# A state-space decoder step: VectorE's table, power and scan operands moved from SBUF to PSUM, 12 output tables on VectorE

## The chip, the cores and the metric

One core of one Trainium2 chip runs the whole step as one program. The metric is the device time of that program in microseconds: the median of three runs, with the lowest and the highest beside it. Times inside the program come from one profiled execution.

## What is computed

One inference step of a two-layer decoder on 320 tokens (256 of a prompt, 8 sequences of 8 new tokens). Layer 1 is a state-space layer with complex diagonal states (64 groups of 16 channels, 64 states each) and a squared-ReLU MLP; then one shared key/value projection; layer 2 is block attention and another MLP. The part that the change touches is the state-space layer:

```
dt = exp(log_dt);  A = exp((lam_re + i lam_im) dt)          # per group and state
Bbar = (A - 1) / lam * B                                    # complex, 64 states x 16 channels per group
x[t] = A x[t-1] + Bbar u[t]                                 # scan over time, start state given for the samples
y[t] = Re(C x[t]) + d u[t];   y = gelu(y);   h += glu(y W)
```

After it come only large matrix products (the gated unit, MLP, keys, queries, values, attention, output, MLP).

## The kernel before

**Blocks.** Time is cut into 40 blocks (`NK`) of 8 steps (`L`), 32 of the prompt and 8 of the samples. Three things are built from A, B and C for each of 8 sets `hb` of 4 group pairs: the input table (powers of A times B, `table` with `ADD`, lines 293 to 306, tiles `eb` or `fb`), the kernel inside a block (C times the input table, spread to a Toeplitz matrix), and the output table (powers of A times C, `ftab`, line 311, tiles `fb`). A table is five tensor-by-tensor instructions: three products (lines 299 to 301, one of them into a scratch tile) and a difference and a sum (302, 304 or 305).

**Sets.** The loop over `hb` (line 382) goes in the order 0, 1, 2, 3, 6, 4, 5, 7. For sets 0 to 5 VectorE builds the input table; for 6 and 7 GpSimd does. TensorE transposes the table (line 404), ScalarE copies it out of PSUM (`et`, 405), TensorE multiplies it with the tokens (413) and ScalarE copies the block inputs out (`e`, 416). Three more steps trail behind by one, two and three places (`chunks`): `kernel` (340 to 344), `toeplitz` (353, 354) and `within` (364), whose result either stays in its PSUM bank (`HELD`) or is copied to `ya` (370).

**Powers and scan.** VectorE then completes the powers A^1 to A^8 (`PW`, lines 423 to 426) and, by squaring, A^8, A^16, A^24 and A^32 (`AW`, with a sign-changed copy `AP_`, lines 435 to 440). The scan (lines 449 to 486) runs in two halves of 16 group pairs: `cstep` (455 to 458, four instructions of 128x256) three times, then a serial loop of seven times four instructions of 128x32 (473 to 476, on `z`), then `cstep` three more times; the results go to `st`, the states at the start of each block. GpSimd meanwhile builds the output tables of `FP` (26 of 32 group pairs); VectorE builds those of `FL` (6) after the scan. GpSimd also makes the final states of the samples (`finished`), clears a tile (682) and makes two weight remainders (547).

**The end of the part.** TensorE multiplies `st` with the output tables (line 504), adding to the held banks; for sets not held VectorE adds `ya` (512); ScalarE applies the GELU (513), TensorE transposes (519), ScalarE and VectorE split the result in two (522, 523), and the gated unit's products begin (567 to 569).

**What sets the order.** The program is written in one order and each engine's own queue comes out of a list scheduler that weighs waits; `issue_after` adds a condition. Each engine works its queue strictly in that order. PSUM has eight banks of 128x512, handed out by `Slots`, oldest freed first. One of them (`PF`, line 278) already holds a copy of the first eight powers for the tables of sets 1 to 5; all else that VectorE reads there lies in SBUF.

Of the kernel before, what the change touches and what calls it, by code (L numbers as in the profile page):

```python
# [16 lines left out]
AF = mybir.ActivationFunctionType  # L17
# [14 lines left out]
NEG = -1e30  # L32
FP = (0, 4), (4, 4), (8, 4), (12, 4), (16, 4), (20, 4), (24, 2)
FL = (26, 2), (28, 4)
HELD = (3, 4, 5, 6, 7)
WARM = 18, 25
# [4 lines left out]
MUL, ADD, SUB, MAX, MIN = ALU.mult, ALU.add, ALU.subtract, ALU.max, ALU.min  # L41
# [21 lines left out]
def body(ctx: ExitStack, tc: tile.TileContext, I, O):  # L63
# [22 lines left out]
    tz_, st, ya, yb = (slot(n_, 2624) for n_ in ("tz", "st", "ya", "yb"))  # L86
    Y = [ya[:, i * 512:(i + 1) * 512] for i in range(5)]
    eb = [wpool.tile([128, 1024], F32, name=f"eb{i}", tag="wr") for i in range(4)]
# [153 lines left out]
    def cmulv(out, x, y, ypm, n, w=scr, o2=512):  # L242

        d = [[64, n], [32, 2], [1, 32]]
        t1, t2 = fv(w, 0, d), fv(w, o2, d)
        V.tensor_tensor(t1, fv(x, 0, d), fv(y, 0, [[0, n], [0, 2], [1, 32]]), op=MUL)
        V.tensor_tensor(t2, fv(x, 32, [[64, n], [-32, 2], [1, 32]]), fv(ypm, 0, [[0, n], [32, 2], [1, 32]]), op=MUL)
        return V.tensor_tensor(fv(out, 0, d), t1, t2, op=ADD)


    pm(p1, PW[:, 64:128])
# [25 lines left out]
    cmulv(px[:, 256:512], px[:, 0:256], PW[:, 256:320], p4, 4)  # L277
    PF = B.get()
    e8 = [[64, 8], [1, 32]]
    summed = V.tensor_tensor(fv(px, 512, [[32, 8], [1, 32]]), fv(px, 0, e8), fv(px, 32, e8), op=ADD)  # L280
    A.activation(PF, px[:, 0:512], AF.Copy)


# [23 lines left out]
    xb, xc = (bre, bim, bsum), (cre, cim, csum)  # L307
    prod = yb[:, 0:512]
    held = {}

    def ftab(eng, gp, n, k1):

        return table(eng, fb[gp // 8][:, gp % 8 * 256:(gp % 8 + n) * 256], k1, PW, 64, pws, xc, gp, SUB, n)
# [7 lines left out]

    last = table(V, eb[0], prod, px, 0, px[:, 512:768], xb, 0, ADD)
    P.tensor_tensor(w0, rs0, rs0, op=MUL)
# [57 lines left out]
    for n_, hb in enumerate(order):  # L381
# [6 lines left out]
        if hb < 6:  # L388
            ebt = eb[hb % 4]
            if n_:  # L390
                last = table(V, ebt, prod, PF, 0, px[:, 512:768], xb, g0, ADD)
        else:
            ebt = fb[3][:, (hb - 6) * 1024:(hb - 5) * 1024]
            with tc.issue_after(scaled.ins):
                early = table(P, ebt, scr, px, 0, px[:, 512:768], xb, g0, ADD)
# [24 lines left out]

    B.put(PF)

    with tc.issue_after(last.ins):
        cmulv(PW[:, 192:256], PW[:, 128:192], PW[:, 64:128], p1, 1, fin, 256)
        cmulv(PW[:, 320:576], PW[:, 64:320], PW[:, 256:320], p4, 4, fin, 256)
        powers = V.tensor_tensor(fv(pws, 0, [[32, 8], [1, 32]]), fv(PW, 64, e8), fv(PW, 96, e8), op=ADD)

    for n_ in range(8, 11):
        chunks(n_)
    with tc.issue_after(early.ins):  # L430
        for gp, n in FP:
            tabled = ftab(P, gp, n, scr)
    with tc.issue_after(powers.ins):

        V.tensor_copy(AW[:, 0:64], PW[:, 512:576])
        pm(AP_[:, 0:64], AW[:, 0:64])
        cmulv(AW[:, 64:128], AW[:, 0:64], AW[:, 0:64], AP_[:, 0:64], 1, fin, 256)
        pm(AP_[:, 64:128], AW[:, 64:128])
        cmulv(AW[:, 128:256], AW[:, 0:128], AW[:, 64:128], AP_[:, 64:128], 2, fin, 256)
        pm(AP_[:, 128:256], AW[:, 128:256], 2)  # L440

# [6 lines left out]
    for g0 in (0, 16):  # L448
        def ev(j, sw=False, n=8, step=4):
            return fv(e, g0 * 80 + j + 640 * sw, [[640 * (1 - 2 * sw), 2], [NK, 16], [step, n]])  # L450

        def cstep(out, x, xs, m, add, eng=V, w=sc):

            ta, tb = fv(w, 0, d8), fv(w, 256, d8)
            eng.tensor_tensor(ta, fv(AW, (m - 1) * 64 + g0, [[0, 2], [1, 16], [0, 8]]), x, op=MUL)  # L455
            eng.tensor_tensor(tb, fv(AP_, (m - 1) * 64 + g0, [[32, 2], [1, 16], [0, 8]]), xs, op=MUL)  # L456
            eng.tensor_tensor(ta, ta, add, op=ADD)  # L457
            return eng.tensor_tensor(out, ta, tb, op=ADD)  # L458
# [11 lines left out]
        for s in range(1, 8):  # L470
            o = fv(z, (s + 1) * 32, cc) if s < 7 else fv(fin, g0, ca)
            ta, tb = (fv(sc, (s % 2) * 64 + k_, cc) for k_ in (0, 32))
            V.tensor_tensor(ta, fv(AW, 192 + g0, [[0, 2], [1, 16]]), fv(z, s * 32, cc), op=MUL)
            V.tensor_tensor(tb, fv(AP_, 192 + g0, ca), fv(z, s * 32 + 16, [[-16, 2], [1, 16]]), op=MUL)
            V.tensor_tensor(ta, ta, fv(e, g0 * 80 + 4 * s + 3, [[640, 2], [NK, 16]]), op=ADD)
            V.tensor_tensor(o, ta, tb, op=ADD)
# [7 lines left out]
        with tc.issue_after(tabled.ins):  # L484
            finished = cstep(fv(fin, 64 + g0 * 8, c8), fv(h0, g0 * 8, c8), fv(h0, 256 + g0 * 8, [[-256, 2], [8, 16], [1, 8]]), 1,
                             ev(32, n=8, step=1), P, scr)
    nc.sync.dma_start(O["fin"], fin)


    with tc.issue_after(scanned[0].ins):  # L490
        for gp, n in FL:
            ftab(V, gp, n, prod)
    ga = [slot("ga"), slot("gb")]
# [692 lines left out]
```

## Time and profile before

| | |
|---|---|
| median of 3 runs | 838.82 us (837.09 to 841.32) |
| the profiled execution | 841.09 us, its span 839.3 us |
| busy share of the span | TensorE 92%, VectorE 63%, ScalarE 44%, GpSimd 13% |
| TensorE's mean granted clock | 0.955 of full |
| chain that ended last | TensorE 79%, VectorE 16%, transfers 2% |

Shares of busy time are means over stages with different limits: the stretches have to be read apart. A row of the timeline names the start and the duration in microseconds, the engine, the line, what is written and read, and how many equal instructions it merges; in brackets stands the idle time ahead and what ended it. A duration runs to the end of the writing, and the next instruction can start a little earlier.

### The profile page before, as it was taken

The numbers are of one execution on the slowest core, as the hardware profiler recorded it, in microseconds if no ns is written. First come the engines' busy times: TensorE is split into PE (matmuls) and PEld (weight loads), VectorE is DVE, ScalarE is ACT, GpSimd is POOL, SyncE is SP. The second block draws the span as 40 slices with busy tenths as digits, with TensorE's granted clock in tenths as the row PEclk, the third lists the DMA queues.
The fourth block names the chain that finished last, engine by engine and source line by source line (L and its number), as shares of the span: only waits on it lengthen the run. The fifth ranks groups of instructions, "written<-read, shape, count | busy, mean of one in ns | idle before, by whom it ended". The sixth has DMA issues, their size and how long they took to land.

```text
span 839.3 us, 14630 instructions
## 1 busy us (share of the span) xinstructions
PE 768.9 (92%) x5939; PEld 724.8 (86%) x5940; DVE 527.6 (63%) x900; ACT 370.3 (44%) x651; POOL 108.4 (13%) x123
## 2 busy tenths in 40 slices
PE   7594158999999999999999998997999999999998
PEld 3473047999999999999999995676999999999997
DVE  8999998566666664454566855555775555543432
ACT  4261134444555553333365456545555555433220
POOL 5969803000000000000000221000000000000000
PEclk9697588999999999999999998998999999999999
DMA  4011004343544446644554695872444444444430
GB/s 174 1 53 51 0 15 160 130 149 128 165 147 150 150 147 199 203 149 150 179 200 173 207 245 199 297 283 88 151 151 150 153 151 148 152 164 157 164 119 16
DMA packets 34771, 123.11 MB, mean 147 GB/s; under 512 B 4432, under 2 KB 5712, under 8 KB 34448
## 3 DMA queue, kind: packets, MB, share of 16 engines
q1 hardware_dynamic: 32832, 114.32, 40.6%
q0 software_dynamic: 1872, 7.87, 3.5%
q8 instruction: 46, 0.75, 0.4%
q14 instruction: 21, 0.17, 0.1%
HBM read 116.63 MB, written 5.54 MB: 146 GB/s over the span
## 4 chain that ended last, share of the span: by engine, by line
PE 79%; DVE 16%; DMA 2%; ACT 1%; issue 1%; POOL 0%; DVEq 0%; ACTq 0%; POOLq 0%
PE banks L567 24%; PE banks L569 24%; PE banks L568 24%; DVE so L455 1%; DVE so L457 1%; DVE yb L300 1%; DMA sscr<-raw 1%; DVE so L456 1%; PE banks L963 1%; DVE eb L304 1%; PE banks L895 1%; DVE e L458 1%; PE banks L858 1%; PE banks L886 1%; PE banks L926 1%
## 5 line engine op out<-in xcount | busy, mean ns | idle before, releaser
L552 DVE TENSOR_TENSOR wl<-wr,wh 128x1024 fp32r<-128x1024 f32 x172 | 210.6, 1225 | 183.5 <-ACT wh L549 183.1
L549 ACT ACTIVATE wh<-wr 128x1024 fp32r<-128x1024 f32 x172 | 182.0, 1058 | 211.8 <-PE banks L568 169.2
L567 PE MATMUL banks<-hid,wh 128*128 128x320 f32 x512 | 157.7, 308 | 0.0
L568 PE MATMUL banks<-hid,wh 128*128 128x320 f32 x512 | 157.7, 308 | 0.0
L569 PE MATMUL banks<-hid,wl 128*128 128x320 f32 x512 | 157.7, 308 | 0.0
L567 PEld LDWEIGHTS banks<-hid,wh 128*128 128x128 f32 x512 | 96.1, 188 | 0.0
L568 PEld LDWEIGHTS banks<-hid,wh 128*128 128x128 f32 x512 | 96.1, 188 | 0.0
L569 PEld LDWEIGHTS banks<-hid,wl 128*128 128x128 f32 x512 | 96.1, 188 | 0.0
L567 PE MATMUL banks<-mh,wh 128*128 128x320 f32 x256 | 79.2, 309 | 0.3 <-ACT mh L580 0.3
L567 PE MATMUL banks<-nh,wh 128*128 128x320 f32 x256 | 79.1, 309 | 0.0
L568 PE MATMUL banks<-nl,wh 128*128 128x320 f32 x256 | 78.9, 308 | 0.0
L569 PE MATMUL banks<-nh,wl 128*128 128x320 f32 x256 | 78.9, 308 | 0.0
L568 PE MATMUL banks<-ml,wh 128*128 128x320 f32 x256 | 78.7, 308 | 0.0
L569 PE MATMUL banks<-mh,wl 128*128 128x320 f32 x256 | 78.7, 308 | 0.0
L577 ACT ACTIVATE hid<-rl 128x320 fp32r<-128x320 f32 x64 | 30.2, 471 | 85.4 <-DVE rl L626 84.0
L578 DVE TENSOR_TENSOR hid<-rl,hid 128x320 fp32r<-128x320 f32 x64 | 31.4, 490 | 32.9 <-ACT hid L577 32.9
L567 PEld LDWEIGHTS banks<-mh,wh 128*128 128x128 f32 x256 | 48.1, 188 | 0.6 <-ACT mh L580 0.6
L567 PEld LDWEIGHTS banks<-nh,wh 128*128 128x128 f32 x256 | 48.1, 188 | 0.1
L568 PEld LDWEIGHTS banks<-nl,wh 128*128 128x128 f32 x256 | 48.1, 188 | 0.1
L568 PEld LDWEIGHTS banks<-ml,wh 128*128 128x128 f32 x256 | 48.1, 188 | 0.1
L569 PEld LDWEIGHTS banks<-nh,wl 128*128 128x128 f32 x256 | 48.1, 188 | 0.0
L569 PEld LDWEIGHTS banks<-mh,wl 128*128 128x128 f32 x256 | 48.0, 188 | 0.0
(332 smaller groups left out, 1475.3 us busy)
## 6 DMA issues: line engine op xcount, KB each, us to landing
wr<-in_w SPq DMA_DIRECT2D x176, 512.0 KB, 3.3
kc<-in_ck SPq DMA_DIRECT2D x16, 512.0 KB, 5.0
vc<-in_cv SPq DMA_DIRECT2D x16, 512.0 KB, 5.3
xu<-in_xu SPq DMA_DIRECT2D x2, 640.0 KB, 5.3
xt<-in_xt POOLq DMA_DIRECT2D x1, 1280.0 KB, 5.9
out_k<-raw POOLq DMA_DIRECT2D x2, 640.0 KB, 4.8
kt<-out_k POOLq DMA_DIRECT2D x4, 320.0 KB, 10.2
out_y<-dn SPq DMA_DIRECT2D x8, 160.0 KB, 1.8
```

Of the source, the lines that this page charges most:

```text
L300: eng.tensor_tensor(fv(k1, 0, t3), fv(ws, g0, [[1, n], [32, 8], [0, 16]]), fv(x[0], g0 * 16, xv), op=MUL)
L304: return eng.tensor_tensor(fv(dst, 128, d2), fv(k1, 0, t2), fv(dst, 128, d2), op=ADD)
L455: eng.tensor_tensor(ta, fv(AW, (m - 1) * 64 + g0, [[0, 2], [1, 16], [0, 8]]), x, op=MUL)
L456: eng.tensor_tensor(tb, fv(AP_, (m - 1) * 64 + g0, [[32, 2], [1, 16], [0, 8]]), xs, op=MUL)
L457: eng.tensor_tensor(ta, ta, add, op=ADD)
L549: A.activation(hi, raw, AF.Copy)
L552: V.tensor_tensor(lo, raw, hi.bitcast(F32), op=SUB)
L567: T.matmul(out, h_, xh, start=(first and k == 0), stop=False)
L568: T.matmul(out, h_, xl, start=False, stop=False)
L569: T.matmul(out, l_, xh, start=False, stop=(last and k == 7))
L577: A.activation(h_.bitcast(F32R), src, AF.Copy)
L578: V.tensor_tensor(l_.bitcast(F32R), src, h_, op=SUB)
```

## The change

1. Two more PSUM banks are taken for the length of the part, beside `PF`: `PS`, with a copy of the summed powers and of the four factors that the powers need, and `K1`, the scratch of VectorE's products. The input tables of sets 1 to 5, the last powers (`cmulp`) and the scan then have one operand of each instruction in PSUM. The first input table gets only its scratch there.
2. The squared powers' copies and sign changes go from VectorE to ScalarE (`pma`), which writes them twice, to SBUF for GpSimd and to PSUM (`AWP`, `APP`, in the bank of `PF`) for VectorE. The squarings read the PSUM copies.
3. `HELD` shrinks from five sets to three (4, 5, 7 of 8); sets 3 and 6 are copied to `ya` and added back by VectorE.
4. The output tables are cut 20 for GpSimd and 12 for VectorE (26 and 6 before).

```diff
-FP = (0, 4), (4, 4), (8, 4), (12, 4), (16, 4), (20, 4), (24, 2)
-FL = (26, 2), (28, 4)
-HELD = (3, 4, 5, 6, 7)
+FP = (0, 4), (4, 4), (8, 4), (12, 4), (16, 4)
+FL = (20, 4), (24, 4), (28, 4)
+HELD = (4, 5, 7)
...
+    def cmulp(out, x, y, ypm, n):
+
+        d = [[64, n], [32, 2], [1, 32]]
+        t1, t2 = fv(K1, 0, d), fv(so_, 512, d)
+        V.tensor_tensor(t1, fv(x, 0, d), fv(y, 0, [[0, n], [0, 2], [1, 32]]), op=MUL)
+        V.tensor_tensor(t2, fv(x, 32, [[64, n], [-32, 2], [1, 32]]), fv(ypm, 0, [[0, n], [32, 2], [1, 32]]), op=MUL)
+        return V.tensor_tensor(fv(out, 0, d), t1, t2, op=ADD)
+
+    def pma(dst, src, n=1):
+
+        A.activation(fv(dst, 0, [[64, n], [1, 32]]), fv(src, 32, [[64, n], [1, 32]]), AF.Copy, scale=-1.0)
+        return A.activation(fv(dst, 32, [[64, n], [1, 32]]), fv(src, 32, [[64, n], [1, 32]]), AF.Copy)
...
-    PF = B.get()
+    PF, PS, K1 = B.get(), B.get(), B.get()
...
+    A.activation(PS[:, 0:256], px[:, 512:768], AF.Copy)
+    for i, src in enumerate((PW[:, 64:128], p1, PW[:, 256:320], p4)):
+        A.activation(PS[:, 256 + i * 64:320 + i * 64], src, AF.Copy)
...
-    last = table(V, eb[0], prod, px, 0, px[:, 512:768], xb, 0, ADD)
+    last = table(V, eb[0], K1, px, 0, px[:, 512:768], xb, 0, ADD)
...
-                last = table(V, ebt, prod, PF, 0, px[:, 512:768], xb, g0, ADD)
+                last = table(V, ebt, K1, PF, 0, PS, xb, g0, ADD)
...
-        cmulv(PW[:, 192:256], PW[:, 128:192], PW[:, 64:128], p1, 1, fin, 256)
-        cmulv(PW[:, 320:576], PW[:, 64:320], PW[:, 256:320], p4, 4, fin, 256)
+        cmulp(PW[:, 192:256], PW[:, 128:192], PS[:, 256:320], PS[:, 320:384], 1)
+        cmulp(PW[:, 320:576], PW[:, 64:320], PS[:, 384:448], PS[:, 448:512], 4)
...
+    AWP, APP = PF[:, 0:256], PF[:, 256:512]
+    A.activation(AW[:, 0:64], PW[:, 512:576], AF.Copy)
+    pma(AP_[:, 0:64], PW[:, 512:576])
+    A.activation(AWP[:, 0:64], PW[:, 512:576], AF.Copy)
+    pma(APP[:, 0:64], PW[:, 512:576])
     with tc.issue_after(powers.ins):
-
-        V.tensor_copy(AW[:, 0:64], PW[:, 512:576])
-        pm(AP_[:, 0:64], AW[:, 0:64])
-        cmulv(AW[:, 64:128], AW[:, 0:64], AW[:, 0:64], AP_[:, 0:64], 1, fin, 256)
-        pm(AP_[:, 64:128], AW[:, 64:128])
-        cmulv(AW[:, 128:256], AW[:, 0:128], AW[:, 64:128], AP_[:, 64:128], 2, fin, 256)
-        pm(AP_[:, 128:256], AW[:, 128:256], 2)
+        cmulp(AW[:, 64:128], AW[:, 0:64], AWP[:, 0:64], APP[:, 0:64], 1)
+        A.activation(AWP[:, 64:128], AW[:, 64:128], AF.Copy)
+        pma(APP[:, 64:128], AW[:, 64:128])
+        cmulp(AW[:, 128:256], AW[:, 0:128], AWP[:, 64:128], APP[:, 64:128], 2)
+        A.activation(AWP[:, 128:256], AW[:, 128:256], AF.Copy)
+        pma(APP[:, 128:256], AW[:, 128:256], 2)
...
-        def cstep(out, x, xs, m, add, eng=V, w=sc):
-
-            ta, tb = fv(w, 0, d8), fv(w, 256, d8)
-            eng.tensor_tensor(ta, fv(AW, (m - 1) * 64 + g0, [[0, 2], [1, 16], [0, 8]]), x, op=MUL)
-            eng.tensor_tensor(tb, fv(AP_, (m - 1) * 64 + g0, [[32, 2], [1, 16], [0, 8]]), xs, op=MUL)
+        def cstep(out, x, xs, m, add, eng=V):
+
+            aw, ap, wa, wb = (AWP, APP, K1, sc) if eng is V else (AW, AP_, scr, scr)
+            ta, tb = fv(wa, 0, d8), fv(wb, 256, d8)
+            eng.tensor_tensor(ta, fv(aw, (m - 1) * 64 + g0, [[0, 2], [1, 16], [0, 8]]), x, op=MUL)
+            eng.tensor_tensor(tb, fv(ap, (m - 1) * 64 + g0, [[32, 2], [1, 16], [0, 8]]), xs, op=MUL)
...
-            ta, tb = (fv(sc, (s % 2) * 64 + k_, cc) for k_ in (0, 32))
-            V.tensor_tensor(ta, fv(AW, 192 + g0, [[0, 2], [1, 16]]), fv(z, s * 32, cc), op=MUL)
-            V.tensor_tensor(tb, fv(AP_, 192 + g0, ca), fv(z, s * 32 + 16, [[-16, 2], [1, 16]]), op=MUL)
+            ta, tb = fv(K1, (s % 2) * 64, cc), fv(sc, (s % 2) * 64, cc)
+            V.tensor_tensor(ta, fv(AWP, 192 + g0, [[0, 2], [1, 16]]), fv(z, s * 32, cc), op=MUL)
+            V.tensor_tensor(tb, fv(APP, 192 + g0, ca), fv(z, s * 32 + 16, [[-16, 2], [1, 16]]), op=MUL)
...
-            ftab(V, gp, n, prod)
+            ftab(V, gp, n, K1)
+    B.put(PF, K1)
```

**How the order moves, VectorE between the powers and the scan.** Names: `par` holds `PW`, `AW` and `AP_`; `banks` is PSUM; `so` is the scratch; `e` holds the block inputs. In the kernel before, copies and sign changes stand among the squarings, and the first `cstep` (455 to 458) is mixed in:

```order
L435 COPY par<-par 128x64
L239 TENSOR_SCALAR par<-par 128x32 [waits DVE_49]
L240 COPY par<-par 128x32
L246 TENSOR_TENSOR par<-par 128x64
L247 TENSOR_TENSOR par<-par 128x64 [waits DVE_49]
L455 TENSOR_TENSOR so<-par,e 128x256 [waits Activation_49]
L248 TENSOR_TENSOR par<-par 128x64 [waits DVE_49]
L456 TENSOR_TENSOR so<-par,e 128x256
```

In the changed kernel the same place reads:

```order
L441 TENSOR_TENSOR px<-par 128x256 [waits DVE_49]
L254 TENSOR_TENSOR banks<-par,banks 128x64 [waits Activation_49]
L255 TENSOR_TENSOR so<-par,banks 128x64
L256 TENSOR_TENSOR par<-banks,so 128x64 [waits DVE_49]
L254 TENSOR_TENSOR banks<-par,banks 128x128 [waits DVE_49,Activation_49]
L255 TENSOR_TENSOR so<-par,banks 128x128
L256 TENSOR_TENSOR par<-banks,so 128x128 [waits DVE_49]
L477 TENSOR_TENSOR banks<-banks,e 128x256 [waits DVE_49,Activation_49]
L478 TENSOR_TENSOR so<-banks,e 128x256
```

The copies and sign changes have left VectorE, and each squaring and the first `cstep` now wait for ScalarE (`Activation_49`).

**ScalarE at that place.** These are the changed kernel's rows around the last copies of the powers (457 to 460 and the two lines of `pma`, 260 and 261), among the copies that serve TensorE (`et`, `e`, `ktp`, `tz`, `ya`); this stretch belongs to set 5, the seventh in the loop. In the kernel before, only the copies for TensorE stand here.

```order
L457 ACTIVATE banks<-par 128x64 [waits DVE_49,Activation_49]
L260 ACTIVATE banks<-par 128x32 [waits Activation_49]
L386 ACTIVATE ya<-banks 128x512 [waits PE_49]
L421 ACTIVATE et_91<-banks 128x512 [waits PE_49] x2
L261 ACTIVATE banks<-par 128x32 [waits Activation_49]
L432 ACTIVATE e<-banks 128x4x2x40 [waits PE_49]
L360 ACTIVATE ktp<-banks 128x128 [waits PE_49]
L460 ACTIVATE banks<-par 128x128 [waits DVE_49,Activation_49]
L370 ACTIVATE tz<-banks 128x4x8x16 [waits PE_49] x2
L260 ACTIVATE banks<-par 128x2x32 [waits Activation_49]
L261 ACTIVATE banks<-par 128x2x32 [waits Activation_49]
```

The last two rows write what the first `cstep` waits for; ahead of them in ScalarE's queue stand copies that wait for TensorE's products of the seventh set, the two `tz` among them.

## Rows read from the trace of the kernel before

**Rows 1.** The table of stretches (busy time of each engine with its count of instructions, then the granted clock as a share of full, the share of the transfers and GB/s): TensorE, its weight loads, VectorE, ScalarE, GpSimd.
```profile
31.00:52.00 21.00, 20.16 (x264) 15.86 (x264) 21.00 (x26) 10.57 (x22) 15.62 (x10) 0.85 0.10 30
54.00:60.00 6.00, 6.00 (x106) 4.78 (x104) 5.97 (x7) 3.53 (x9) 6.00 (x6) 1.00 0.01 3
...
54.00:101.50 47.50, 18.87 (x300) 14.74 (x296) 46.88 (x55) 10.43 (x22) 45.52 (x41) 0.72 0.07 23
...
160.00:839.30 679.30, 666.77 (x4831) 643.11 (x4829) 382.07 (x633) 313.70 (x545) 18.29 (x40) 0.99 0.50 165
```

**Rows 2.** Timeline of VectorE: one input table while GpSimd works, then the first and the last instruction of a later table, when GpSimd has stopped.
```profile
40.69 0.68 DVE L299 TENSOR_TENSOR eb<-banks,bc 128x512 f32<-128x512 f32 x1
41.29 1.00 DVE L300 TENSOR_TENSOR yb<-px,bc 128x512 f32<-128x512 f32 x1
42.21 0.68 DVE L301 TENSOR_TENSOR eb<-banks,bc 128x512 f32<-128x512 f32 x1
42.81 0.99 DVE L302 TENSOR_TENSOR eb<-yb,eb 128x512 f32<-128x512 f32 x1
43.72 1.77 DVE L304 TENSOR_TENSOR eb<-yb,eb 128x512 f32<-128x512 f32 x1
...
48.90 0.68 DVE L299 TENSOR_TENSOR eb<-banks,bc 128x512 f32<-128x512 f32 x1
...
51.29 0.68 DVE L304 TENSOR_TENSOR eb<-yb,eb 128x512 f32<-128x512 f32 x1
```

**Rows 3.** Timeline of GpSimd: the last instruction of its own input tables, the first of the output tables, the first of a later table of 512 columns, and the first of the table behind that.
```profile
44.89 1.73 POOL L304 TENSOR_TENSOR fb<-scr,fb 128x512 f32<-128x512 f32 x1
53.84 1.34 POOL L299 TENSOR_TENSOR fb<-par,ktp 128x512 f32<-128x512 f32 x1 [7.22 <-DVE par L248]
...
86.72 1.10 POOL L299 TENSOR_TENSOR fb<-par,ktp 128x512 f32<-128x512 f32 x1
...
92.33 0.64 POOL L299 TENSOR_TENSOR fb<-par,ktp 128x256 f32<-128x256 f32 x1
```

**Rows 4.** Timeline of VectorE: the third product, the difference and the sum of the first input table.
```profile
25.96 2.01 DVE L301 TENSOR_TENSOR eb<-px,bc 128x512 f32<-128x512 f32 x1
27.90 1.58 DVE L302 TENSOR_TENSOR eb<-yb,eb 128x512 f32<-128x512 f32 x1
29.41 1.59 DVE L304 TENSOR_TENSOR eb<-yb,eb 128x512 f32<-128x512 f32 x1
```

**Rows 5.** Timeline of VectorE: the scan's first half (second `cstep`, copy and first step of the serial loop) beside GpSimd's work, and the same places of the second half, with its first and last instruction.
```profile
72.73 1.56 DVE L455 TENSOR_TENSOR so<-par,e 128x256 f32<-128x256 f32 x1
...
77.20 1.57 DVE L458 TENSOR_TENSOR e<-so 128x256 f32<-128x256 f32 x1
...
84.57 1.01 DVE L469 COPY px<-e 128x32 f32<-128x32 f32 x1
85.62 1.19 DVE L473 TENSOR_TENSOR so<-par,px 128x32 f32<-128x32 f32 x1
...
109.00 0.62 DVE L455 TENSOR_TENSOR so<-par,e 128x256 f32<-128x256 f32 x1
...
116.10 0.19 DVE L469 COPY px<-e 128x32 f32<-128x32 f32 x1
116.33 0.19 DVE L473 TENSOR_TENSOR so<-par,px 128x32 f32<-128x32 f32 x1
...
127.44 0.64 DVE L458 TENSOR_TENSOR st<-so 128x256 f32<-128x256 f32 x1
```

**Rows 6.** Timeline of TensorE: the first products of the set loop; then the products 353 before the `tz` copies of set 5, the seventh in the loop.
```profile
31.05 1.54 PE L404 MATMUL banks<-cst,eb 128*128 128x128 f32 x6 [0.24 <-DVE eb L304]
...
64.35 1.07 PE L353 MATMUL banks<-cst,ktp 128*128 128x128 f32 x8
```

**Rows 7.** Timeline of ScalarE: a small copy, a copy into PSUM, a copy out of it, and the two `tz` copies of set 5.
```profile
9.39 0.21 ACT L225 ACTIVATE tz<-tz 128x32 f32<-128x32 f32 x1
20.53 0.60 ACT L281 ACTIVATE banks<-px 128x512 f32<-128x512 f32 x1 [0.16 <-DVE px L248]
31.99 0.60 ACT L405 ACTIVATE et<-banks 128x512 f32<-128x512 f32 x1 [10.86 <-PE banks L404]
65.66 1.08 ACT L354 ACTIVATE tz<-banks 128x512 f32<-128x512 f32 x2
```

**Rows 8.** Timeline of VectorE and GpSimd at the output tables after the scan, and the adds behind them.
```profile
127.91 2.52 DVE L299 TENSOR_TENSOR fb<-par,ktp 128x256 f32<-128x256 f32 x1
130.35 2.56 DVE L300 TENSOR_TENSOR yb<-px,bc 128x256 f32<-128x256 f32 x1
132.83 0.41 DVE L301 TENSOR_TENSOR fb<-par,bc 128x256 f32<-128x256 f32 x1
...
136.24 0.68 DVE L305 TENSOR_TENSOR fb<-fb,yb 128x512 f32<-128x512 f32 x1
136.84 1.88 DVE L512 TENSOR_TENSOR ya<-banks,ya 128x512 f32<-128x512 f32 x3
...
127.49 5.13 POOL L547 TENSOR_TENSOR wl<-wr,wh 128x1024 fp32r<-128x1024 f32 x2
```

**Rows 9.** Timeline of TensorE: the last group of output products, and the gated unit's product from which it runs without a gap.
```profile
136.37 2.56 PE L504 MATMUL banks<-fb,st 64*64 64x128 f32 x38 [1.68 <-DVE fb L302]
...
144.63 0.31 PE L567 MATMUL banks<-zh,wh 128*128 128x320 f32 x1
```

More of the change, by code (lines that the diff above doesn't have):

```diff
@@ L86, in body @@
     tz_, st, ya, yb = (slot(n_, 2624) for n_ in ("tz", "st", "ya", "yb"))
-    Y = [ya[:, i * 512:(i + 1) * 512] for i in range(5)]
+    Y = {q: ya[:, i * 512:(i + 1) * 512] for i, q in enumerate((0, 1, 2, 3, 6))}
     eb = [wpool.tile([128, 1024], F32, name=f"eb{i}", tag="wr") for i in range(4)]
@@ L307, in body @@
     xb, xc = (bre, bim, bsum), (cre, cim, csum)
-    prod = yb[:, 0:512]
     held = {}
@@ L419, in body @@
         chunks(n_)
-    B.put(PF)
     with tc.issue_after(last.ins):
-        cmulv(PW[:, 192:256], PW[:, 128:192], PW[:, 64:128], p1, 1, fin, 256)
-        cmulv(PW[:, 320:576], PW[:, 64:320], PW[:, 256:320], p4, 4, fin, 256)
+        cmulp(PW[:, 192:256], PW[:, 128:192], PS[:, 256:320], PS[:, 320:384], 1)
+        cmulp(PW[:, 320:576], PW[:, 64:320], PS[:, 384:448], PS[:, 448:512], 4)
         powers = V.tensor_tensor(fv(pws, 0, [[32, 8], [1, 32]]), fv(PW, 64, e8), fv(PW, 96, e8), op=ADD)
+    B.put(PS)
     for n_ in range(8, 11):
@@ L485, in body @@
             finished = cstep(fv(fin, 64 + g0 * 8, c8), fv(h0, g0 * 8, c8), fv(h0, 256 + g0 * 8, [[-256, 2], [8, 16], [1, 8]]), 1,
-                             ev(32, n=8, step=1), P, scr)
+                             ev(32, n=8, step=1), P)
     nc.sync.dma_start(O["fin"], fin)
```

## The prediction, as put on record before the run

> **What bounds the kernel now.** I read the stretches first. From 160 us to the end TensorE is busy 666.77 of 679.30 us, and the change touches nothing there [rows 1]. From 54 to 101.5 us it is busy only 18.87 of 47.50, while VectorE is busy 46.88 and GpSimd 45.52: in the state-space part the end is set by VectorE. So the question is how much earlier TensorE can start its long run, which is at 144.63 us now.
>
> Second, the timeline of VectorE beside GpSimd. In one and the same input table, instructions that read one operand from PSUM take 0.68 us (299, 301) and those with both operands in SBUF take 1.00, 0.99 and 1.77 (300, 302, 304) [rows 2]. Once GpSimd has ended, at 44.89 + 1.73 = 46.6 us [rows 3], the same 304 takes 0.68 [rows 2]. So an instruction of VectorE that reads two operands from SBUF waits for the one that GpSimd has running, and GpSimd's wait for VectorE's; one with an operand in PSUM does not. The scan pays this most: beside GpSimd a step's 455 takes 1.56 us and the small 473 takes 1.19; alone they take 0.62 and 0.19 [rows 5].
>
> Third, who is next. Between 31 and 52 us TensorE is busy 20.16 of 21.00 us, between 54 and 60 all of 6.00 [rows 1]: while the tables are made, TensorE is a bound of its own, only that nobody waits for it now.
>
> **The change, part by part.**
>
> *First input table.* Its three products still read two SBUF operands each and keep their 2.01 us. The difference and the sum now read `K1`: 0.60 from start to start (48.90 to 51.29 is four steps, 2.39 us [rows 2]) in place of 1.58 and 1.59. The table ends at 25.96 + 2.01 + 2 x 0.60 = 29.2 us in place of 29.41 + 1.59 = 31.0 [rows 4]. TensorE starts its run 1.8 us earlier (31.05 now [rows 6]).
>
> *Input tables of sets 1 to 5 and the last powers.* They fall from 4.7 us each (40.69 to 43.72 + 1.77, less the overlap) to 5 x 0.60 = 3.0 [rows 2], so VectorE is through with tables and powers at some 47 us and not at 54. I cost this gain at nothing: the scan cannot use it, because of the next part.
>
> *Squared powers on ScalarE.* This is the wait that the change adds. The first `cstep` needs the last sign-changed copy, and in ScalarE's queue that stands behind the two `tz` copies of the seventh set, which wait for TensorE's products 353 of that set. In the profile those products start at 64.35 [rows 6] and the copies end at 65.66 + 1.08 = 66.74 us [rows 7]. TensorE has hardly a gap to lose before it, so this point moves by the 1.8 us of the start: 64.9. Behind it come two small copies, 0.21 us each [rows 7], to 65.4. The other small copies and those into `PS`, about a dozen and a half at 0.2, cost ScalarE 3 to 4 us, of which most falls into its idle time (it is busy 3.53 of 6.00 [rows 1]); I take 0.6. The scan starts at **66.0**; ends 64.4 (TensorE's remaining 0.84 us of gaps between 31 and 52 goes too) and 70 (all copies on the path, and waits for banks). VectorE will stand idle for some 18 us before it, with the squarings waiting in its queue, and nobody else waits for those. GpSimd's `finished` needs them too, but only after its tables.
>
> *Scan.* Each instruction now has one operand in PSUM, so both halves should run as the second does now, when GpSimd is idle: 109.00 to 127.44 + 0.64 = 128.08, 19.1 us [rows 5]. In the first half the copy 469 has no PSUM operand and keeps its 1.01 against 0.19: 0.8 more [rows 5]. End of the scan: 66.0 + 19.9 + 19.1 = **105.0**, where it was 128.08.
>
> *Output tables.* GpSimd builds 20 of 32, five tables at 92.33 - 86.72 = 5.6 us [rows 3], from some 47 to 75 us; nobody reads them before 86. VectorE builds 12: 15 instructions of 0.60 where ten smaller ones stood. GpSimd's two remainders still start 0.6 us before the end of the scan (127.49 against 128.08), at 104.4, run 5.13 us, and hold VectorE's first two instructions, which read two SBUF operands: these end at 130.35 + 2.56 = 132.91 now [rows 8], 0.3 behind the remainders. With 0.6 in place of 0.33 for each, the pair ends at 104.4 + 5.13 + 0.25 + 0.6 = 110.4. Thirteen more at 0.60 end at **118.2**, where 136.24 + 0.68 = 136.92 stands now [rows 8]: of the scan's 23.1 us, 4.4 are given back here.
>
> *Held banks.* Two sets more are added by VectorE, 1.88 / 3 = 0.6 us each [rows 8], and one of them now stands between the last products and the GELU. The tail, 136.92 to 144.63 = 7.7 us [rows 8, 9], becomes 7.7 + 2 x 0.6 + 0.6 = 9.5. TensorE runs from 127.7 on: **16.9 us** earlier.
>
> *What an operand in PSUM costs.* Reading shows no price: 299 and 301 take 0.68 with it and 304 takes 0.68 without [rows 2]. VectorE writes to PSUM nowhere in this trace, and 52 of the scan's 104 instructions now do. The nearest rows are ScalarE's, 0.60 us for 512 columns into PSUM and 0.60 out of it [rows 7]: no price, and no gain. At the other end, the 0.08 us by which 0.68 exceeds 0.60, writing that lies beside the next instruction, could come free of that cover: 52 x 0.08 = 4.2 us. I take 0.02 each, 1.0 us, near ScalarE's rows. [...]
>
> **Sum.** 16.9 - 1.0 = 15.9 us off the profiled execution's 841.09, 825.2. That execution stands 2.3 us above the median of the runs, 838.82, so I forecast **823 us** (818 to 828 with the ends of the scan's start, 64.4 and 70, and of the PSUM writes, 0 and 4.2).
>
> **The rivals.**
>
> *A. PSUM operands are dearer than the rows show* (for: the serial loop is a chain of small instructions, where a fixed price counts in full; against: 0.68 both ways). At twice the 0.08 us, 0.16 on 52 instructions, 8.3 us are lost and the time is 830.
>
> *B. The change does not free the scan.* Beside GpSimd the trace shows just one form that is free: first operand in PSUM, second in SBUF, result in SBUF. Half of the scan writes to PSUM; if such instructions still waited, the scan would run contended until GpSimd has ended (75 us for its tables, about 5 more for `finished`): 14 us at 0.62 / 1.56 of the pace [rows 5] lose 8.4, and the time is 831. For: nothing was seen. Against: what waits is a second read from SBUF, which they don't make.
>
> *C. Five banks do not feed TensorE; slower than before.* `PF`, `PS` and `K1` leave five banks for the seven uses that each set makes in turn, against seven before. If a TensorE product had to wait out the copy that empties its bank, 0.60 us [rows 7], at each of 7 x 6 handovers up to the seventh set, TensorE would lose 25 us, the scan would start at 91 and the time would be 848. It decides from 0.38 us a handover, where the scan starts at 82 and all 15.9 us are gone. A third of it gives 831 and half of it 836, no change. For: TensorE has no slack there. Against: in the order a bank comes up again five uses later, mostly long after its copy. [...]
>
> [...]
>
> **Chances.** Forecast 0.70; A 0.12; B 0.06; C 0.08, of which 0.05 lies at 836 and 0.03 is slower than before; D 0.04. The range **817 to 831** takes in the forecast, A, D and most of B: D and A are the ends, and C is what is left out. A measurement tells 0.5%, 4.2 us, from no change: faster than 834.6 is 0.92 (forecast, A, B, D), the same 0.05, slower 0.03.
>
> **What would show it.** Right: the scan's first `cstep` starts near 66 us, released by ScalarE, after an idle stretch of VectorE of some 18 us; its instructions take 0.62 while GpSimd is busy, and the small ones 0.19; the scan ends near 105, VectorE's last table near 118, and TensorE runs without a gap from about 128. TensorE is as busy between 29 and 65 as now. Wrong: `cstep` instructions of 1.5 us beside GpSimd (B); 0.35 and more for the small ones (A); TensorE waiting for ScalarE at each set and a start of the scan beyond 75 (C). If the scan starts near 66 and TensorE still starts near 140, the loss is in the tables after the scan or in the tail, and my terms for those are wrong.

## The result and the profile after

The changed kernel takes **818.98 us** (median of 4 runs, 817.52 to 819.66) against 839.13 of the kernel before in the same session: 0.9757 of it, 95% interval 0.9728 to 0.9786. Forecast were 823 us (817 to 831). The profiled execution took 819.45 us, its span is 817.7.

The stretches, read as in [rows 1] (TensorE, its weight loads, VectorE, ScalarE, GpSimd, granted clock, transfers):

```profile
31.00:52.00 21.00, 18.95 (x275) 14.43 (x272) 15.07 (x31) 10.79 (x24) 16.59 (x15) 0.94 0.16 52
54.00:66.00 12.00, 12.00 (x185) 9.54 (x181) 2.25 (x8) 9.59 (x28) 12.00 (x11) 1.00 0.15 45
66.00:85.00 19.00, 10.36 (x159) 8.36 (x158) 18.00 (x53) 11.17 (x19) 13.69 (x16) 0.90 0.09 28
```

VectorE is nearly idle from 54 to 66 us (2.25 of 12.00) and TensorE is without a gap there. That is the added wait of the prediction. From 66 on VectorE is the bound again (18.00 of 19.00 us busy to 85).

VectorE's timeline: the end of the first table and one `K1` product of the second (lines 316 to 321 are 299 to 304 of before), the waits before the scan, then the scan (477 to 480 are 455 to 458, 491 is 469, 495 is 473):

```profile
28.21 0.68 DVE L321 TENSOR_TENSOR eb<-banks,eb 128x512 f32<-128x512 f32 x1
28.80 0.67 DVE L316 TENSOR_TENSOR eb<-banks,bc 128x512 f32<-128x512 f32 x1
29.40 0.68 DVE L317 TENSOR_TENSOR banks<-banks,bc 128x512 f32<-128x512 f32 x1
...
43.16 0.67 DVE L321 TENSOR_TENSOR eb<-banks,eb 128x512 f32<-128x512 f32 x1
...
57.39 0.23 DVE L254 TENSOR_TENSOR banks<-par,banks 128x64 f32<-128x64 f32 x1 [11.22 <-ACT banks L261]
...
61.34 0.30 DVE L254 TENSOR_TENSOR banks<-par,banks 128x128 f32<-128x128 f32 x1 [3.33 <-ACT banks L261]
...
65.10 0.64 DVE L477 TENSOR_TENSOR banks<-banks,e 128x256 f32<-128x256 f32 x1 [2.95 <-ACT banks L261]
...
66.82 0.63 DVE L480 TENSOR_TENSOR e<-banks,so 128x256 f32<-128x256 f32 x1
...
72.28 1.04 DVE L491 COPY px<-e 128x32 f32<-128x32 f32 x1
73.36 0.20 DVE L495 TENSOR_TENSOR banks<-banks,px 128x32 f32<-128x32 f32 x1
73.46 0.18 DVE L496 TENSOR_TENSOR so<-banks,px 128x32 f32<-128x32 f32 x1
...
84.94 0.61 DVE L477 TENSOR_TENSOR banks<-banks,e 128x256 f32<-128x256 f32 x1
...
103.10 0.63 DVE L480 TENSOR_TENSOR st<-banks,so 128x256 f32<-128x256 f32 x1
```

Against [rows 4, 5]: the first table ends at 28.9 and not 31.0; a `cstep` row beside GpSimd takes 0.6 us and not 1.5, a row of the serial loop 0.20 and not 1.19. The two halves take 19.8 us (65.10 to 84.94) and 18.8 (84.94 to 103.73). Three waits for ScalarE's line 261, 17.5 us in all, lie before the first `cstep`. In the scan only 491, a copy from SBUF to SBUF, still waits for GpSimd (1.04 us, 0.19 in the second half), which is in the last of its output tables by then:

```profile
72.00 1.27 POOL L319 TENSOR_TENSOR fb<-scr,fb 128x512 f32<-128x512 f32 x1
73.23 1.29 POOL L322 TENSOR_TENSOR fb<-fb,scr 128x512 f32<-128x512 f32 x1
74.60 0.63 POOL L477 TENSOR_TENSOR scr<-par 128x256 f32<-128x256 f32 x1
```

ScalarE ahead of that first `cstep`: the `tz` copies of set 5, then the two rows that it waits for.

```profile
63.60 1.08 ACT L370 ACTIVATE tz<-banks 128x512 f32<-128x512 f32 x2
64.57 0.24 ACT L260 ACTIVATE banks<-par 128x64 f32<-128x64 f32 x1
64.84 0.23 ACT L261 ACTIVATE banks<-par 128x64 f32<-128x64 f32 x1
```

The tail on VectorE (output tables 316 to 322, adds 535), with TensorE's product after which it runs without a gap:

```profile
103.57 2.47 DVE L316 TENSOR_TENSOR fb<-par,ktp 128x512 f32<-128x512 f32 x1
105.96 2.83 DVE L317 TENSOR_TENSOR banks<-px,bc 128x512 f32<-128x512 f32 x1
...
115.92 0.67 DVE L322 TENSOR_TENSOR fb<-fb,banks 128x512 f32<-128x512 f32 x1
116.51 2.47 DVE L535 TENSOR_TENSOR ya<-banks,ya 128x512 f32<-128x512 f32 x4
```
```profile
124.97 0.31 PE L590 MATMUL banks<-zh,wh 128*128 128x320 f32 x1
```

TensorE's long run starts at 124.97 and not at 144.63 [rows 9], 19.7 us earlier; the median fell by 20.2.

### The profile page after: what moved, and what is told of

It is laid out like the page before. It is cut to its first block, busy times and chain, and to the rows that moved or that the text cites. A ratio compares the mean times of both kernels' runs of the same rounds, so it can differ in the third digit from the quotient of the medians.

```text
span 817.7 us, 14636 instructions
## 1 busy us (share of the span) xinstructions
PE 767.6 (94%) x5939; PEld 725.3 (89%) x5940; DVE 490.9 (60%) x900; ACT 374.5 (46%) x670; POOL 90.2 (11%) x113
## 4 chain that ended last, share of the span: by engine, by line
PE 83%; DVE 10%; DMA 3%; ACT 2%; issue 1%; POOL 0%; ACTq 0%; DVEq 0%; POOLq 0%
PE banks L590 25%; PE banks L592 24%; PE banks L591 24%; PE banks L429 1%; DMA sscr<-raw 1%; PE banks L986 1%; DMA qt<-qscr 1%; DVE banks L477 1%; DVE banks L479 1%; PE banks L420 1%; PE banks L881 1%; DVE banks L317 1%; PE banks L909 1%; DVE so L478 1%; PE banks L918 1%
```

## The experiments

The theory was the prediction's: the scan is freed because a VectorE instruction with one operand in PSUM does not wait for GpSimd (P); the input tables' gain is hidden (H); the new wait is ScalarE's queue (A); after the scan VectorE's output tables, the first two instructions of them beside GpSimd's remainders, give time back (G). Each edit is on the changed kernel unless said otherwise, and "TensorE's run" is its start without a gap.

**The changed kernel again**, as the measure for the others.

> The changed kernel itself, beside the other three on one chip, so that they can be compared with it and not only with the kernel before. Every theory: 819 us, 0.976 of the kernel before; first cstep of the scan near 65.1 us, scan through at 103.7, TensorE without a gap from 125.0.

819.59 us (817.79 to 822.22), 0.9769 of the kernel before (0.9739 to 0.9798). In this execution the copy 491 took 0.68 us, where the other one shows 1.04.

**1. The scan alone back in SBUF.**

```diff
-            aw, ap, wa, wb = (AWP, APP, K1, sc) if eng is V else (AW, AP_, scr, scr)
+            aw, ap, wa, wb = (AW, AP_, sc, sc) if eng is V else (AW, AP_, scr, scr)
...
-            ta, tb = fv(K1, (s % 2) * 64, cc), fv(sc, (s % 2) * 64, cc)
+            ta, tb = fv(sc, (s % 2) * 64, cc), fv(sc, (s % 2) * 64 + 32, cc)
```

The serial loop reads `AW` and `AP_` too, and ScalarE's last sign changes go there.

> The changed kernel with the scan alone taken back to SBUF (factors AW and AP_, both scratch products in sc); the tables and powers keep their PSUM operands, the 20/12 split and three held sets stay. Theory P (a VectorE instruction with two SBUF operands waits for GpSimd's running one): the scan still starts near 65.1, but its first three csteps take 6.0 us each and not 2.4 until GpSimd is through, which itself is slowed to about 84; first half ends near 96.5, second near 115.6, 11.9 us later than in the changed kernel: 831 us (828 to 834). Rival T (the gain comes from GpSimd's smaller share and the new order, the operands of the scan matter little): scan through by 106, 819 to 822 us.

828.82 us, 0.9883 (0.9857 to 0.9909). VectorE's second `cstep`:

```profile
67.04 1.28 DVE L477 TENSOR_TENSOR so<-par,e 128x256 f32<-128x256 f32 x1
68.24 1.54 DVE L478 TENSOR_TENSOR so<-par,e 128x256 f32<-128x256 f32 x1
69.69 1.72 DVE L479 TENSOR_TENSOR so<-so,e 128x256 f32<-128x256 f32 x1
71.44 1.60 DVE L480 TENSOR_TENSOR e<-so 128x256 f32<-128x256 f32 x1
```

6.0 us from this `cstep` to the next, as expected. The scan started at 62.31 and not at 65.1 (one of its products at 56.94), which is why the time came out 2 us below 831: in SBUF the first `cstep` is not tied to ScalarE's last sign changes, whose columns it does not read; in the changed kernel it waits for them, perhaps since they lie in the same bank (no run separates that). It ended at 113.20, 9.5 us later than in the changed kernel; the time is 9.2 us longer. P holds, T falls.

But 828.82 us is still 9.9 below the kernel before (838.75, measured beside it), so the scan's operands are only about half of the change's gain. With the scan in SBUF, GpSimd is through at 84.4 us and not at 103.5, and VectorE no longer makes the copies of the squared powers; how the other half divides among these and the rest of the change, no run shows.

**2. The input tables alone back in SBUF.**

```diff
-    last = table(V, eb[0], K1, px, 0, px[:, 512:768], xb, 0, ADD)
+    last = table(V, eb[0], yb[:, 0:512], px, 0, px[:, 512:768], xb, 0, ADD)
...
-                last = table(V, ebt, K1, PF, 0, PS, xb, g0, ADD)
+                last = table(V, ebt, yb[:, 0:512], PF, 0, px[:, 512:768], xb, g0, ADD)
```

> The changed kernel with the six input tables alone taken back to their SBUF scratch and SBUF sums; powers and scan keep PSUM. Theory H (the tables' gain is hidden behind TensorE and ScalarE, only the first table counts): tables through near 52 us and not 43.8, VectorE idles 7 us less before the scan, the scan starts 1.8 to 2.1 us later since the first table ends at 31.0 and not 28.9: 821 us (820 to 822). Rival V (VectorE's tables set the scan's start): 8 us later, 827 us.

826.75 us, 0.9848 (0.9823 to 0.9873): 7 us lost, the number of rival V. But the timeline speaks against V: the tables were through at 52 us, VectorE then still waited 8.4 us in three waits, and the scan started at 63.99, even earlier (here the last sign changes stand ahead of the `tz` copies on ScalarE). The loss is one row of VectorE:

```profile
71.18 8.80 DVE L491 COPY px<-e 128x32 f32<-128x32 f32 x1
80.01 0.20 DVE L495 TENSOR_TENSOR banks<-banks,px 128x32 f32<-128x32 f32 x1
```

Beside it GpSimd worked without a gap, up to the 0.08 us between 79.93 and 80.01, where an instruction needs the result of the one just before it:

```profile
70.87 1.27 POOL L322 TENSOR_TENSOR fb<-fb,scr 128x512 f32<-128x512 f32 x1
72.10 1.10 POOL L318 TENSOR_TENSOR fb<-par,bc 128x512 f32<-128x512 f32 x1
...
77.77 1.11 POOL L318 TENSOR_TENSOR fb<-par,bc 128x512 f32<-128x512 f32 x1
78.82 1.11 POOL L317 TENSOR_TENSOR scr<-px,bc 128x512 f32<-128x512 f32 x1
80.01 1.26 POOL L319 TENSOR_TENSOR fb<-scr,fb 128x512 f32<-128x512 f32 x1
```

The copy was passed over by eight GpSimd instructions. So a new theory, K: the loss is this instruction, and the tables' gain is hidden after all.

**3. The same, with the copy given an operand in PSUM.**

```diff
-        V.tensor_copy(fv(z, 32, cc), fv(e, g0 * 80 + 3, [[640, 2], [NK, 16]]))
+        V.tensor_tensor(fv(z, 32, cc), fv(K1, 480, cc), fv(e, g0 * 80 + 3, [[640, 2], [NK, 16]]), op=ADD)
```

(32 columns of `K1` are set to zero once, before the scan.)

> The kernel with the input tables back in SBUF (which measured 826.75 us and not 821), with one more edit: the scan's small copy of 32 columns from e to z is made by adding zeros that lie in PSUM, so that this instruction too has an operand in PSUM. In that kernel the copy, the scan's only instruction on two SBUF sides, took 8.80 us from 71.18 to 79.98 beside GpSimd, and 1.04 in the changed kernel. Theory K (the whole loss is this one instruction, which GpSimd's row of instructions keeps waiting; the tables' gain itself is hidden): it takes 0.2 us, the scan ends 8.6 us earlier, 818 us (817 to 820). Rival V (the tables are worth those 7 us after all, and the copy only shows a wait that stands there anyway): still 826 us, with the wait on another instruction.

816.77 us, 0.9748 (0.9725 to 0.9772). The row takes 0.21 us, the scan ends at 101.7. K holds, V falls: with the tables in SBUF and the copy's PSUM operand the kernel is not slower than the changed one, so a gain of the tables' part of the change is not seen here. My expectation for 2, that the scan starts 1.8 us later, was wrong too: TensorE's products before the `tz` copies did move by 2.06 us (62.93 to 64.99), but the scan no longer waited for them.

**4. The squared powers made by VectorE.**

```diff
+        V.tensor_copy(AWP[:, 0:64], PW[:, 512:576])
+        V.tensor_copy(AW[:, 0:64], AWP[:, 0:64])
+        pm(APP[:, 0:64], AWP[:, 0:64])
         cmulp(AW[:, 64:128], AW[:, 0:64], AWP[:, 0:64], APP[:, 0:64], 1)
-        A.activation(AWP[:, 64:128], AW[:, 64:128], AF.Copy)
-        pma(APP[:, 64:128], AW[:, 64:128])
+        V.tensor_copy(AWP[:, 64:128], AW[:, 64:128])
+        pm(APP[:, 64:128], AWP[:, 64:128])
...
```

(The same for the columns from 128 on.)

> The changed kernel, but the squared powers and their sign-changed copies for the scan are made by VectorE itself in PSUM (ten small copies and sign changes of 0.1 to 0.2 us on VectorE in place of ScalarE's). Theory A (the scan's start hangs on ScalarE's queue alone, and VectorE's 17.5 us of idle time before it are worth their whole length): scan starts near 49.5, ends near 88, the last table near 101, TensorE without a gap from 109.5: 803.5 us (801 to 808). Rival S (something else stands behind that wait: results of TensorE that the scan reads, or the output products behind TensorE's set loop, which ends at 76.3): under half of it comes through, 811 us or more. Rival C (VectorE's small copies wait for GpSimd, 1.04 us each): scan starts near 58, 812 us.

805.14 us, 0.9594 (0.9568 to 0.9619). The last sign change and the first `cstep`:

```profile
49.96 0.23 DVE L240 COPY banks<-banks 128x64 f32<-128x64 f32 x1
50.30 0.64 DVE L477 TENSOR_TENSOR banks<-banks,e 128x256 f32<-128x256 f32 x1
```

The scan starts 14.8 us earlier than in the changed kernel, and the time falls by 14.5. A holds; S and C fall: copies with one or both sides in PSUM take 0.20 to 0.29 us beside GpSimd.

**5. The remainders ahead of the clearing of `px` in GpSimd's queue.**

```diff
-    cleared = P.memset(px[:, 0:512], 0.0)
+    with tc.issue_after(rests[-1].ins):
+        cleared = P.memset(px[:, 0:512], 0.0)
```

(`rests` collects the remainders.)

> The changed kernel with one row moved in GpSimd's queue: the clearing of px (which must wait for the end of the scan) behind the remainders of panels 2 and 3 and not ahead of them, so that these run from 80.1 to 85.2 in GpSimd's idle time and no longer beside VectorE's first two output-table instructions. Theory G (the prediction's 4.4 us given back there are real, but behind them TensorE's output products, 4.11 + 9.65 us for 152 of them, bound the tail): the pair takes 1.2 us and not 5.2, the last table ends near 112.6, but TensorE's run starts only 3 to 3.5 us earlier: 816.3 us (815 to 817). Rival N (nothing waits for those two: products or VectorE's adds set the tail): 819 us. Rival F (all of it comes through): 815.0 us.

816.47 us, 0.9737 (0.9714 to 0.9759), 3.1 us below the changed kernel's 819.59; the intervals overlap. The number is as expected, the way there is not. Only the first remainder moved (to 80.36); the second ran at 102.90, since its tile comes free at the end of the scan. 316 took 0.68 us and not 2.47, 317 still 2.83:

```profile
102.61 0.68 DVE L316 TENSOR_TENSOR fb<-par,ktp 128x512 f32<-128x512 f32 x1
103.21 2.83 DVE L317 TENSOR_TENSOR banks<-px,bc 128x512 f32<-128x512 f32 x1
```
```profile
102.90 2.58 POOL L571 TENSOR_TENSOR wl<-wr,wh 128x1024 fp32r<-128x1024 f32 x1 [20.18 <-issue]
```

And the copy 491 took 0.19 here (it ran from 72.12 to 72.31 and met a gap in GpSimd's work, 72.24 to 72.32), so that the scan ended at 102.77, 1.0 earlier. From the end of the scan to TensorE's run it is 19.45 us and not 21.24: 1.79 less, all of what 316 lost. So G's bound by TensorE's output products did not hold at this size.

**6. All output tables on GpSimd.**

```diff
-FP = (0, 4), (4, 4), (8, 4), (12, 4), (16, 4)
-FL = (20, 4), (24, 4), (28, 4)
+FP = (0, 4), (4, 4), (8, 4), (12, 4), (16, 4), (20, 4), (24, 4), (28, 4)
+FL = ()
```

> The changed kernel with all 32 output tables on GpSimd and none on VectorE; the rest stays. GpSimd builds eight tables at 5.65 us from 45.8 to 91.5 and is through with its small work near 97, before the scan ends at 103.6. Theory G (behind the tables TensorE's output products bound the tail): VectorE's tables, 13 us from 103.6 to 116.6, fall away, yet TensorE's run starts only some 3 us earlier: 816 us (815 to 818). Rival F (the twelve tables are the path and cost their 13 us): 806 us. Rival N (a longer GpSimd slows the scan, which now has it beside both halves): 819 us or more.

830.05 us, 0.9898 (0.9878 to 0.9919). The time fits rival N, but again it is one row: 491 took 16.68 us, from 72.45 to 89.13, through 15 GpSimd instructions:

```profile
72.45 16.68 DVE L491 COPY px<-e 128x32 f32<-128x32 f32 x1
```

Is it the copy, or any instruction of VectorE with two sides in SBUF?

**7. The same, with a maximum on two SBUF operands for the copy.**

```diff
-        V.tensor_copy(fv(z, 32, cc), fv(e, g0 * 80 + 3, [[640, 2], [NK, 16]]))
+        e3 = fv(e, g0 * 80 + 3, [[640, 2], [NK, 16]])
+        V.tensor_tensor(fv(z, 32, cc), e3, e3, op=MAX)
```

> The kernel with all 32 output tables on GpSimd (830.05 us, where the copy of 32 columns from e to z took 16.68 us, from 72.45 to 89.13), with that copy made by a tensor_tensor, the maximum of e and e: the same columns, both operands and the result in SBUF. Theory L (only the copy is passed over; a tensor_tensor with two SBUF operands gets in behind the GpSimd instruction that is running, as in every such row of the other profiles, where the longest is 1.8 us): it takes up to 1.4 us, the scan ends near 103.6, TensorE's run starts some 3 us earlier than in the changed kernel since its output products bound the tail: 816 us. Rival M (any single instruction of that sort is passed over while GpSimd's instructions follow one another without a gap): 16 us again, 830 us. Rival F (the tables taken from VectorE are the path): 806 us.

829.43 us, 0.9888 (0.9871 to 0.9906). VectorE, then GpSimd at the end of the wait:

```profile
72.09 16.91 DVE L492 TENSOR_TENSOR px<-e 128x32 f32<-128x32 f32 x1
```
```profile
86.76 1.10 POOL L318 TENSOR_TENSOR fb<-par,bc 128x512 f32<-128x512 f32 x1
87.82 1.10 POOL L317 TENSOR_TENSOR scr<-px,bc 128x512 f32<-128x512 f32 x1
89.00 1.26 POOL L319 TENSOR_TENSOR fb<-scr,fb 128x512 f32<-128x512 f32 x1
```

It ends at 89.00, in the 0.08 us between 317 and 319, the only such gap in those 17 us. M holds, L falls: it is not the copy.

**8. The same, with zeros from PSUM** (the edit of 3).

> The kernel with all 32 output tables on GpSimd, with the copy of 32 columns made by adding zeros that lie in PSUM (it took 16.68 us there as a copy and 16.91 as a maximum on SBUF operands). Theory M (a single instruction with both operands in SBUF is passed over for as long as GpSimd's instructions follow without a gap, and that wait was all of the loss): the instruction takes 0.2 us, the scan ends near 102.8 and the time falls by 16.5 us, to 813.3 us (812 to 816), some 4 to 6 below the changed kernel, since TensorE's output products bound the tail once VectorE's tables are gone. Rival N (a GpSimd that is busy beside both halves slows the scan in another way): 820 us or more. Rival F (the twelve tables were the path in full): 806 us.

814.66 us, 0.9707 (0.9685 to 0.9729): the row takes 0.21 us, the scan ends at 102.8, and 15.4 us come back. So a GpSimd that is busy to 97 us costs the scan nothing else. VectorE's tables (13 us from 103.57 to 116.59) are gone, yet the median is only 4.9 us below the changed kernel's (the profiled execution, 812.47, is the fastest of five), an estimated 0.8 of it by the copy (1.04 - 0.21): TensorE's output products and transposes now fill the tail, with 2.0 us of gaps between 101.78 and 117.95 (F falls).

**9. Only the scan's factors in PSUM, its scratch in SBUF.**

```diff
-            aw, ap, wa, wb = (AWP, APP, K1, sc) if eng is V else (AW, AP_, scr, scr)
+            aw, ap, wa, wb = (AWP, APP, sc, sc) if eng is V else (AW, AP_, scr, scr)
```

(The serial loop likewise.)

> The changed kernel with the scan's scratch products back in SBUF (sc for K1); its factors AWP and APP stay in PSUM, and everything else. Theory P, instruction by instruction: the two products of a cstep read one SBUF operand and stay at 0.6 us beside GpSimd, the two additions now read two and take some 1.5, so a cstep takes about 4.1 us and not 2.4 (with all of the scan in SBUF it was 6.0) and a step of the serial loop 1.3 and not 0.71, until GpSimd is through near 82.5: scan through some 6 us later, 825 us (822 to 827). Rival (the factors alone free the scan): 819 us. Rival (one instruction with two SBUF operands holds the whole cstep to GpSimd's pace): 6 us a cstep, 829 us or more.

826.68 us, 0.9862 (0.984 to 0.9883), within the 822 to 827 of P, by another path. VectorE's first `cstep`, and GpSimd at the end of its wait:

```profile
64.72 0.62 DVE L477 TENSOR_TENSOR so<-banks,e 128x256 f32<-128x256 f32 x1 [2.95 <-ACT banks L261]
65.27 0.60 DVE L478 TENSOR_TENSOR so<-banks,e 128x256 f32<-128x256 f32 x1
65.78 6.70 DVE L479 TENSOR_TENSOR so<-so,e 128x256 f32<-128x256 f32 x1
72.52 1.61 DVE L480 TENSOR_TENSOR e<-so 128x256 f32<-128x256 f32 x1
```
```profile
70.89 1.11 POOL L317 TENSOR_TENSOR scr<-px,bc 128x512 f32<-128x512 f32 x1
72.08 1.56 POOL L319 TENSOR_TENSOR fb<-scr,fb 128x512 f32<-128x512 f32 x1
```

In this `cstep` the products go free (0.62 and 0.60 us) and the additions wait, as P has it. But the first addition waits 6.70 us, to GpSimd's gap at 72.0; then the next addition gets in behind one instruction (1.61), and GpSimd's two take 1.56. In the next `cstep`, beside GpSimd's instructions of 128x256, the additions take 0.65 and 0.93.

**10. Edits 3, 4 and 5 together** (on the changed kernel, with its tables in PSUM).

> Three edits of the changed kernel together: squared powers made by VectorE (that alone: 805.14 us), the small copy by an addition with zeros in PSUM, and GpSimd's two remainders ahead of the clearing of px. If theories A, K and G hold and add up: scan from 50.5, through near 88, last table near 97, TensorE's run from 106.5: 801 us (799.5 to 802.5). Rival (the three gains lie beside one another, so that the last two add nothing): 805 us.

801.71 us, 0.9559 (0.954 to 0.9579): the gains add up, 17.9 us below the changed kernel where 14.5 from experiment 4, 1.8 from 5 and 0.8 for the copy make 17.1 (an estimate). The interval overlaps that of experiment 4 alone; what speaks against the rival is the profile, where TensorE's run starts at 108.46 and not at 111.08 as in 4. It was expected at 106.5: the scan ends 1.0 us later than expected (89.01), and the second remainder still holds 317 (2.83 us).

**11. The same, GpSimd making the remainders of panels 1 and 2.**

```diff
-            eng, after = (V, scanned[0]) if i < 2 else (P, finished)
+            eng, after = (P, finished) if i in (1, 2) else (V, scanned[0])
```

> The kernel with the three edits together (801.71 us), where GpSimd's second remainder still ran at 89.15 beside VectorE's tables since its tile only comes free at the end of the scan. Here GpSimd makes the remainders of panels 1 and 2 and VectorE those of 0 and 3. Theory G (TensorE's output products bound the tail, the tables only partly): the tables end 2.2 us earlier, near 97.9, TensorE's run starts 1 to 1.8 us earlier: 800.2 us (799.5 to 801). Rival (VectorE's tables are the bound): 799.5 us. Rival (nothing waits for them): 801.7 us.

801.13 us, 0.9548 (0.9529 to 0.9566), the fastest of all. In the profile both remainders lie before 85.2, 317 takes 0.69, and from the end of the scan to TensorE's run it is 17.29 us, 2.16 less than in 5: again all of it. The 0.6 us between 10 and 11 are within their intervals; what is shown is the profile.

## Why the prediction held, step by step

- **First table.** 29.2 forecast, 28.9 measured. TensorE's products before the `tz` copies moved by 1.4 us (64.35 to 62.93), where 1.8 were forecast.
- **Tables hidden.** Right in its result: with them in SBUF and the copy's PSUM operand the kernel is no slower (experiment 3).
- **The wait for ScalarE.** Forecast a start of the scan at 66.0 after some 18 us of idle time; measured 65.10 and 17.5. It stood where it was put: experiment 4 takes it away and the start falls by 14.8 us.
- **Scan.** 39.0 us forecast for both halves, 38.6 measured. That the operands free its instructions is shown by experiments 1 and 9; in time they are 9.2 us of the change's 20 (experiment 1).
- **The copy 469.** Forecast 0.8 us more, measured 0.85: **right by luck**. The row of before (1.01 us) comes from a stretch in which VectorE asks again and again; here it asks alone. The same instruction at the same place took 0.19, 0.68, 1.04, 1.11, 8.80 and 16.68 us in the kernels above. In the changed kernel it comes when GpSimd is in its last output table, so that a wait to the next gap (74.52) would have been 2.2 us (an estimate, 74.52 - 72.28); had it met more tables, as in experiment 6, it could have cost 15.6 us and the time been some 835 (an estimate, 819 + 15.6), no change. The sum had no term for where GpSimd stands at that moment.
- **Output tables.** The pair held by the remainders was to end 5.4 us after the scan, and ends 5.06 after (108.79); the last table was to end at 118.2, and does at 116.59. Of the scan's gain 4.4 us were to be given back here, and 4.0 were (12.86 us from the end of the scan to the last table, 8.84 before [rows 5, 8]). But 3.8 of that is the tables' number and size: 13 instructions behind the pair take 7.80 us, where eight, three of them of half the size, took 4.01. The wait for the remainders is no new cost: the pair ended 4.83 us after the scan before the change too. So the 1.79 and 2.16 us of experiments 5 and 11 come from a wait that both kernels have, and not out of the 4.4, as my expectation for 5 put it.
- **Held banks.** 1.8 us more of tail were forecast; it grew by 0.7 (116.59 to 124.97, 8.4 us). Four adds (535) lie beside TensorE's last output products.
- **PSUM's price.** 1.0 us forecast, none measured: 0.20 and 0.18 us for small instructions that read PSUM, 0.19 and 0.18 without, and 0.71 us for a step of the serial loop both ways.

The forecast was 4 us too high. TensorE's run came 3.8 us earlier than the 15.9 of the sum: 1.6 by the end of the tables (0.9 of it the start of the scan), 1.1 by the tail, 1.0 by PSUM's price.

Of the rivals, A and B fell with the rows of the scan. C fell: TensorE was busy 12.00 of 12.00 us from 54 to 66 with five banks. Its mechanism shows once, between 31 and 52 us: products 356 waited 0.54 us for ScalarE's copy 432, whose result they do not read. D, the low end of the range at 817 us, stands for a higher granted clock in TensorE's first sets, and no run shows that term: the clock was 0.94 and not 0.85 from 31 to 52 us, but TensorE had new gaps there (18.95 of 21.00 us busy; three waits for ScalarE's copies `et`, 1.4 us, and the one of C), and the scan started at 65.10.

## What to carry to other kernels

When operands are moved so that one engine no longer waits for another, list the instructions that still can: one small copy left behind may wait for one instruction of the other engine or for fifteen (1.04 and 16.68 us here), and its price in a trace where both ask in turn (1.01 us) says nothing of that. Give it a free operand too: with zeros from PSUM it took 0.21 us, and as a copy 0.19 at best. And look at what the moved work now waits for: here small copies on a third engine stood behind a queue that had nothing to do with them, and making them on the idle engine itself was worth 14.5 us, where the whole change brought 20.

## What the runs showed of the hardware that was not expected

A single VectorE instruction with both sides in SBUF, on 128x32 or 128x256 elements, was passed over by six to fifteen GpSimd instructions in a row (6.70, 8.80, 16.68, 16.91 us) and got in at a gap of about 0.08 us in GpSimd's work, each time in its last output table, where 319 follows directly on 317, whose result it needs. Where VectorE sends such instructions one after the other, as in the second `cstep` of experiment 1, they took 1.28 to 1.72 us each and not 0.6, about one GpSimd instruction each, and GpSimd's own grew (318 from 1.11 to 1.52 us). The copy and the tensor_tensor fared alike: the copies took 8.80 and 16.68 us, the tensor_tensors 6.70 and 16.91. One GpSimd instruction beside them lasted 1.10 to 1.30 us, so these four did not wait for one alone.

Open is why the copy got in behind one instruction in three of these profiles (0.68, 1.04, 1.11 us), where GpSimd shows no gap either. In experiment 1, too, two products of the first `cstep`, one behind an idle stretch and one behind instructions with PSUM operands, took 0.89 and 1.59 us, so that sending one after the other is not what decides. The rows at those places look like the ones at which it was passed over, and no run here separates them.
